# Two projections whose low weight halves are made by two engines: GpSimd beside the vector engine

## The chip, the cores and the metric

The kernel runs on one core of one Trainium2 chip. A core has five engines with a queue of instructions each: TensorE (PE in the profile) for matrix products, VectorE (DVE) and ScalarE (ACT) for element-wise work, GpSimd (POOL), and SyncE (SP), which here only issues DMAs. They meet at semaphores. The metric is the device time of one execution in microseconds (us): the median before is 1877.37 us over 3 runs (1877.23 to 1877.73).

## The reference

Two layers run one after the other on a sequence of 256 tokens with 2048 channels, all in float32. Cut to what matters:

```python
def hybrid_layer(x, ...):
    h = rmsnorm(x, norm_g)
    proj = h @ w_in                       # one wide input projection, then split
    y_conv = conv_branch(...) @ w_proj_conv
    y_mla = mla_branch(...) @ w_proj_mla
    y = sigmoid(g_conv) * y_conv + sigmoid(g_mla) * y_mla
    return x + y @ w_out
```

The change touches the two last products of a layer: `w_proj_conv` (2048 by 2048) and `w_out` (2048 by 2048).

## The kernel before

**Split products.** Every float32 product is made of three passes on TensorE in a faster 4-byte format (F32R). An operand is cut into a high part, its rounding to F32R, and a low part, the difference between the value and its high part. With the activations as the stationary operand in parts `sh` and `sl`, and the weights as the moving operand in parts `hi` and `lo`, a block is the sum of `sh*hi`, `sl*hi` and `sh*lo`, accumulated in PSUM (line 314 chooses among them).

**Pieces.** Weights are streamed from memory in pieces, in the order in which they are used (`plan`, lines 161 to 173). A piece holds `KS = 2` K tiles of 128 rows, so it is 128 partitions by 1024 columns for a block 512 columns wide. A piece goes through three engines. `load` (line 182) issues its DMA on SP into a `raw` buffer, of which there are five. `split_hi` (line 191) lets ScalarE write the high part into one of four `hi` buffers. `split_lo` (line 211) lets VectorE write the low part into one of three `lo` buffers, as raw minus high, in one instruction over both K tiles.

**Blocks and slots.** `product` (line 294) makes one block of 256 tokens by 512 columns. In the two products of the change a block has K of 2048, so 16 K tiles and 8 pieces, and a piece feeds 12 matmuls of 512 columns: for two K tiles and two token tiles, the three parts. At piece i the code first issues the high parts up to piece i+3 and the low parts up to piece i+2, then the 12 matmuls of piece i, then `background(n)`, which moves a clock on by one slot and runs the steps that are due in it. `order_of_products` (line 280) puts the four low matmuls of a piece behind its eight high ones; the last piece of a block finishes token tile 0 first, and one piece of a block (`tardy`) takes its late activations in last. Since three `lo` buffers serve, the low part of piece i+2 goes into the buffer that TensorE has finished with at the end of piece i-1.

**Order.** Each engine is wrapped in `InOrder` (line 118), so that it executes in the order in which the code issues. A step that is put off by `at_slot` is issued behind the matmuls of a later piece, and what is issued in a queue before it goes first.

**What GpSimd does.** It issues most of the DMAs that turn a block's result by way of memory: `park` (line 327) writes a tile of 128 by 512 with four DMAs, `fetch` (line 336) reads it back with one, and VectorE finishes with a 32 by 32 transposition. After a block of the convolution's projection (`pconv_evac`) VectorE multiplies and adds two tiles, and each is parked with four DMAs on GpSimd and fetched. After a block of the output projection in the first layer (`wout_evac`) it is the same, with one more DMA for each tile that writes x for the second layer. In the second layer `wout_evac` writes the output with four DMAs on GpSimd instead. In the last block of each product (c = 3) the second tile's park is issued on SP, and the evacuation comes one slot sooner, since the next product waits for it: its last two pieces (pieces 6 and 7 of block 0, where `tardy=6`) read those activations. GpSimd also computes the small inverse square roots of attention, earlier in the layer.

**Names.** In the profile `acc` is a PSUM block; `raw`, `hi`, `lo` are the pieces' buffers; `ycT` are the activations of the convolution's projection, `yT` those of the output projection, `hT` those of the second layer; `gate` and `xres` are tiles on their way out, `turn_d` is the memory they are parked in, `turned` the tile fetched. All instructions have line 126, that of the `InOrder` wrapper.

Of the kernel before, what the change touches and what calls it, by code (L numbers as in the profile page):

```python
# [11 lines left out]
F32 = mybir.dt.float32  # L12
# [93 lines left out]
def blocks_of_layer():  # L106

    s = {"win": [], "wuq": [], "wukv": [], "wpc": [], "wpm": [], "wo": []}
    for kind, i, stream in order_of_layer():
        s[stream].append(DOWN_BLOCKS[i][1] if kind == "down" else 2 * QK if kind == "uq" else 512)  # L110
    return s
# [3 lines left out]
def trunk(ctx: ExitStack, tc: tile.TileContext, xT, x, g_in, pos, win, wuq, wukv, wpc, wpm, wo, cst, rows, invf, out):  # L115
# [19 lines left out]
    pe, vec, act, gps, sp = (InOrder(e) for e in (nc.tensor, nc.vector, nc.scalar, nc.gpsimd, nc.sync))  # L135
# [20 lines left out]

    streams = {"win": (win, 16), "wuq": (wuq, 4), "wukv": (wukv, 4), "wpc": (wpc, 16), "wpm": (wpm, 16), "wo": (wo, 16)}
    taken = {}
    pieces = []

    def plan(layer, stream):
        ap, nk = streams[stream]
        i, at = taken.get((layer, stream), (0, 0))
        n = blocks_of_layer()[stream][i]
        mine = []
        for g in range(nk // KS):
            size = P * KS * n
            pieces.append((ap[layer, at : at + size].rearrange("(p k c) -> p k c", p=P, k=KS), n))
            at += size
            mine.append(len(pieces) - 1)  # L170
        taken[layer, stream] = (i + 1, at)
        return nk, n, mine

# [2 lines left out]
    for l in range(DEPTH):  # L176
        plans.append([(k, i, plan(l, s)) for k, i, s in order_of_layer()])

    loaded, highs, done, blocks_begun = {}, {}, {}, [0]
# [11 lines left out]
    def split_hi(i):  # L191
        if i >= len(pieces) or i in highs:
            return
        load(i)
        highs[i] = split_p.tile([P, KS, pieces[i][1]], F32R, tag="hi", name=f"hi{i}", bufs=4)
        singly = i < 2
        for a in range(0, KS, 1 if singly else KS):
            k = slice(a, a + 1 if singly else KS)

            for step in ("h", "w"):  # L200
                if step == "w":
                    act.copy(highs[i][:, k], loaded[i][:, k])
                    if singly:
                        split_lo(i, k)
                elif i * KS < NCT:
                    for c in range(i * KS + k.start, i * KS + k.stop):
                        first_h(c)
        for a in range(1, LOAD_AHEAD + 1):
            load(i + a)

    def split_lo(i, k=slice(0, KS)):
        if i >= len(pieces) or done.get(i, (0, 0, 0))[2] >= k.stop:
            return
        lo = done[i][1] if i in done else split_p.tile([P, KS, pieces[i][1]], F32R, tag="lo", name=f"lo{i}")
        vec.tensor_sub(lo[:, k], loaded[i][:, k], highs[i][:, k].bitcast(F32))
        done[i] = highs[i], lo, k.stop


# [75 lines left out]
    def product(planned, stat, evacuate, evac_at=EVAC_AT, costs=(0.0, 0.0), before=None, tardy=None):  # L294
        nk, n, mine = planned
        blocks_begun[0] += 1
        pts = [acc_p.tile([P, 512], F32, tag=f"acc{blocks_begun[0] % 2}{t}", name=f"acc{mine[0]}_{t}") for t in range(T)]

        def evac():
            for t in range(T):  # L300
                evacuate(t, pts[t][:, :n])

        for j, i in enumerate(mine):
            for a in range(HI_AHEAD + 1):
                split_hi(i + a)
                if a <= LO_AHEAD:
                    split_lo(i + a)
            hi, lo, _ = done[i]
            if before:
                before(j)  # L310
            for t, kk, part in order_of_products(i, j == len(mine) - 1, j == tardy):
                k = j * KS + kk
                sh, sl = stat(k, t)
                stationary, w = ((sh, hi), (sl, hi), (sh, lo))[part]
                pe.matmul(
                    pts[t][:, :n], stationary, w[:, kk, :],
                    start=k == 0 and part == 0, stop=k == nk - 1 and part == 2,
                )
            if j == len(mine) - 1:
                steps.insert(0, (clock[0] + 1 + evac_at, costs, evac))  # L320
            background(n)
# [1023 lines left out]
```

## Time and profile before

| | |
|---|---|
| median of the runs | 1877.37 us (3 runs, 1877.23 to 1877.73) |
| span of the profiled execution, first to last instruction | 1876.2 us |
| VectorE busy | 1577.1 us (84%) |
| ScalarE busy | 1366.1 us (73%) |
| GpSimd busy | 484.9 us (26%), 942 instructions |
| low parts on VectorE | 690 instructions, 815.2 us |

The profiled execution was not timed apart from its profile; its span of 1876.2 us lies 1.2 us below the median, which also holds what lies around the first and the last instruction. Times in the profile's timelines count from the span's start. A row of a timeline gives start, duration, engine, operation, the tile written and the tiles read, and in square brackets how long the engine sat idle before and what ended the wait. Rows of neighbouring instructions of one kind are merged, with their count behind an x. A matmul of 512 columns is issued 0.227 us after the one before it and shows some 0.39 us, since they overlap in the engine.

### The profile page before, as it was taken

To read this page: it belongs to the slowest core of one execution; us is meant where nothing else is said; L and a number is where in the kernel's file an instruction comes from. 1 tells how busy PE (TensorE), PEld (TensorE's weight loads), DVE (VectorE), ACT (ScalarE), POOL (GpSimd) and SP (SyncE) were. 2 spreads that over 40 slices of the span, in tenths; PEclk is the share of its full clock that TensorE was granted. 3 is DMA by queue.
4 is the path that set the end of the run, shared out by engine and by line. 5 is a ranking of instruction groups with operands and counts; after the bars stand their busy time and mean duration, and the time that the engine had idled before them with its cause. 6 is when DMAs were issued, how large, how long until landed. Compare 5 with 4: busy or idle time off the path is not lost.

```text
span 1876.2 us, 27388 instructions
## 1 busy us (share of the span) xinstructions
PE 1871.3 (100%) x8665; PEld 1584.0 (84%) x8665; DVE 1577.1 (84%) x2426; ACT 1366.1 (73%) x2468; POOL 484.9 (26%) x942
## 2 busy tenths in 40 slices
PE   9999999999999999999999999999999999999999
PEld 8988888888888888888899888888888888888887
DVE  6898988989999988766679899888899999885664
ACT  7678988888888766544557688888888878474442
POOL 1055555432200000122221555555322000001210
PEclk9999999999999999999999999999999999999999
DMA  9677878777755566678876787787777555566774
GB/s 329 217 258 263 273 240 275 262 242 235 244 201 193 196 206 214 210 241 281 288 234 218 249 272 258 261 278 243 245 239 249 190 194 203 209 205 221 239 250 164
DMA packets 140113, 445.06 MB, mean 237 GB/s; under 512 B 23808, under 2 KB 29440, under 8 KB 139968
## 3 DMA queue, kind: packets, MB, share of 16 engines
q1 hardware_dynamic: 106272, 359.89, 57.1%
q0 software_dynamic: 32832, 82.62, 13.5%
q8 instruction: 68, 1.11, 0.2%
q10 hardware_dynamic: 864, 0.80, 0.1%
q14 instruction: 77, 0.63, 0.1%
HBM read 399.18 MB, written 44.04 MB: 236 GB/s over the span
## 4 chain that ended last, share of the span: by engine, by line
PE 100%; DVE 0%; DVEq 0%; issue 0%
PE acc L126 97%; PE s L126 2%; PE o_ps L126 1%; PE warm L126 0%; PE var L126 0%; PE mu L126 0%; DVE xres L126 0%; DVEq L1341 0%; DVE zeros L126 0%
## 5 line engine op out<-in xcount | busy, mean ns | idle before, releaser
L126 ACT CAST hi<-raw 128x1024 fp32r<-128x1024 f32 (+3 forms) x690 | 700.7, 1021 | 408.4 <-PE acc L126 348.1
L126 DVE TENSOR_TENSOR lo<-raw,hi 128x1024 fp32r<-128x1024 f32 (+3 forms) x690 | 815.2, 1183 | 197.7 <-PE acc L126 151.1
L126 PE MATMUL acc<-hi,hT 128*128 128x512 f32 (+2 forms) x1728 | 419.5, 382 | 0.0
L126 PEld LDWEIGHTS acc<-hi,hT 128*128 128x128 f32 x1728 | 319.8, 188 | 59.2
L126 PE MATMUL acc<-hi,h_hi 128*128 128x512 f32 (+2 forms) x864 | 260.7, 383 | 0.0
L126 PE MATMUL acc<-hi,h_lo 128*128 128x512 f32 (+2 forms) x864 | 260.5, 383 | 0.0
L126 ACT ACTIVATE tap<-u_t,cst 128x256 f32<-128x256 f32 x588 | 254.7, 499 | 3.2 <-DVE v_t L126 3.2
L126 PE MATMUL acc<-lo,h_hi 128*128 128x512 f32 (+2 forms) x864 | 229.8, 382 | 0.0
L126 PE MATMUL acc<-lo,hT 128*128 128x512 f32 (+2 forms) x864 | 229.3, 382 | 0.0
L126 DVE TENSOR_TENSOR v_t<-v_t,tap 128x512 f32<-128x512 f32 x294 | 202.2, 688 | 10.4 <-ACT hi L126 0.5
L126 POOL DMA_DIRECT2D turned<-turn_d x88 | 49.1, 558 | 536.6 <-DVE v_t L126 305.4
L126 PEld LDWEIGHTS acc<-hi,h_lo 128*128 128x128 f32 x864 | 161.4, 188 | 30.2
L126 PEld LDWEIGHTS acc<-lo,h_hi 128*128 128x128 f32 x864 | 160.9, 188 | 30.0
L126 PEld LDWEIGHTS acc<-lo,hT 128*128 128x128 f32 x864 | 160.6, 188 | 29.9
L126 PEld LDWEIGHTS acc<-hi,h_hi 128*128 128x128 f32 x864 | 160.4, 188 | 29.0
L126 POOL DMA_DIRECT2D turn_d<-gate x184 | 100.0, 551 | 327.8 <-DVE gate L126 182.9
L126 DVE SCALAR_TENSOR_TENSOR v_t<-u_t,cst,v_t 128x256 f32<-128x256 f32 x372 | 159.7, 480 | 2.3
L126 PE MATMUL acc<-hi,oT 128*128 128x512 f32 x512 | 127.8, 389 | 0.0
L126 PE MATMUL acc<-hi,ycT 128*128 128x512 f32 x512 | 127.7, 389 | 0.0
L126 PE MATMUL acc<-hi,yT 128*128 128x512 f32 x512 | 127.7, 389 | 0.0
L126 PE MATMUL acc<-hi,qkc 128*128 128x512 f32 (+1 forms) x512 | 118.7, 363 | 0.0
L126 PEld LDWEIGHTS acc<-hi,ycT 128*128 128x128 f32 x512 | 96.1, 188 | 19.9
(169 smaller groups left out, 2209.8 us busy)
## 6 DMA issues: line engine op xcount, KB each, us to landing
raw<-in_win SPq DMA_DIRECT2D x382, 512.0 KB, 4.3
raw<-in_wpm SPq DMA_DIRECT2D x64, 512.0 KB, 3.2
raw<-in_wpc SPq DMA_DIRECT2D x64, 512.0 KB, 4.3
raw<-in_wo SPq DMA_DIRECT2D x64, 512.0 KB, 4.8
raw<-in_wukv SPq DMA_DIRECT2D x32, 512.0 KB, 3.6
turned<-turn_d POOLq DMA_DIRECT2D x56, 256.0 KB, 4.8
raw<-in_win SPq DMA_DIRECT2D x32, 384.0 KB, 4.4
raw<-in_wuq SPq DMA_DIRECT2D x32, 384.0 KB, 3.4
```

Source lines behind the costliest of these rows:

```text
L126: ins = getattr(self.engine, name)(*a, **k)
```

## The change

The pieces of `wpc` (the weights of the convolution's projection) and `wo` (those of the output projection) are noted in a set `shared`. For those pieces the low part is made by two instructions of 128 by 512: GpSimd subtracts in the first K tile, VectorE in the second. That is 32 pieces for each of the two products in each of two layers, 128 in all. The other streams' low parts stay one VectorE instruction over both K tiles.

```diff
-    pieces = []
+    pieces, shared = [], set()
...
             mine.append(len(pieces) - 1)
+            if stream in ("wpc", "wo"):
+                shared.add(len(pieces) - 1)
...
         lo = done[i][1] if i in done else split_p.tile([P, KS, pieces[i][1]], F32R, tag="lo", name=f"lo{i}")
-        vec.tensor_sub(lo[:, k], loaded[i][:, k], highs[i][:, k].bitcast(F32))
+        if i in shared:
+            for engine, a in ((gps, 0), (vec, 1)):
+                engine.tensor_sub(lo[:, a], loaded[i][:, a], highs[i][:, a].bitcast(F32))
+        else:
+            vec.tensor_sub(lo[:, k], loaded[i][:, k], highs[i][:, k].bitcast(F32))
         done[i] = highs[i], lo, k.stop
```

The order of instructions on TensorE and ScalarE stays as it was. On VectorE each of the 128 instructions stands where it stood, at half its width. On GpSimd 128 subtractions are new in the queue, among the DMAs: the queue of one block of the output projection in the first layer reads 8 parks, 2 writes of x, 4 subtractions, 2 fetches, 4 subtractions; behind the last block of the convolution's projection it reads 4 parks, 2 subtractions, 2 fetches.

## The prediction

> **What bounds the kernel now.** I read the page first, then what TensorE waits for, then the busy time of the engines in the two stages of the change, then the timeline at their edges.
>
> ```profile
> span 1876.2 us, 27388 instructions
> ...
> PE 1871.3 (100%) x8665; PEld 1584.0 (84%) x8665; DVE 1577.1 (84%) x2426; ACT 1366.1 (73%) x2468; POOL 484.9 (26%) x942
> ...
> PEclk9999999999999999999999999999999999999999
> ...
> PE warm L126 <- DVE zeros L126: 1.2, 1, 1.2
> ...
> 764.90:851.90 87.00, 87.00 (x385) 72.07 (x384) 56.47 (x64) 40.39 (x44) 16.45 (x30) 1.00 0.72 230
> 851.90:939.00 87.10, 87.10 (x386) 72.14 (x385) 56.48 (x71) 44.16 (x64) 23.05 (x42) 1.00 0.85 284
> ```
>
> TensorE is busy 1871.3 of 1876.2 us at the full granted clock (1.00 in both stage rows, whose columns are the stretch, its length, then PE, PEld, DVE, ACT and POOL busy). It waits once in the whole run, 1.2 us at the start; the rest of the 4.9 us without matmuls is the end, behind the last one. The two stages of the first layer, the convolution's projection and the output projection, last 87.0 and 87.1 us with TensorE never idle. So relief of the vector engine buys nothing: whatever changes here shows only if it makes TensorE wait.
>
> **What is removed and what is added.**
>
> ```profile
> L126 DVE TENSOR_TENSOR lo<-raw,hi 128x1024 fp32r<-128x1024 f32 x32 | 38.8, 1221 | 28.2 <-PE acc L126 25.3 <-issue 2.8
> ...
> L126 DVE TENSOR_TENSOR lo<-raw,hi 128x512 fp32r<-128x512 f32 x4 | 2.8, 689 | 0.0
> ```
>
> The groups of VectorE in the first stage, and the same operation at half width elsewhere (name, count, busy us, mean ns, idle time before and its causes): 128 vector instructions shrink from 1.221 to 0.689 us, 68 us of busy time in all. Before, VectorE sat 25.3 of 87 us waiting for TensorE to free a `lo` buffer: it was ahead already. Worth to the path: 0.
>
> GpSimd takes 128 subtractions of 128x512. No such instruction is in the trace; the nearest rows:
>
> ```profile
> L126 POOL TENSOR_TENSOR rsq_t<-r_p x48: 193/313/1173, 133.2 to 1307.4; 128x8 f32<-128x8 f32 x48
> ...
> L126 POOL MEMSET u_t<- 128x60 f32 x16 | 2.7, 167 | 0.3 <-POOLq L1334 0.3
> L126 POOL MEMSET qk_t<- 128x512 f32 x2 | 1.1, 548 | 0.0
> ```
>
> Two memsets give (548-167)/452 = 0.843 ns a column; a two-input operation of 8 columns takes 193 ns when nothing holds it up. From these, estimates for 512 columns: 193 ns and 504 columns at one pass, 0.62 us, the lower bound; two reads in turn, 1.04 us; two reads and a write in turn, 1.47 us, the upper bound. I take 1.25 us, midway between the last two, since no row shows two reads at once, nor that the write can't overlap.
>
> The Trainium skill, GPSIMD Engine Reference, section Elementwise — side-by-side cycle accounting, gives 4497 ns for 2048 columns of a two-input add; a quarter is an estimate of 1.12 us, and by it the sum below would come to about 1878.5. Its section Engine selection speaks against the change: two-input element-wise work belongs on VectorE, GpSimd being about twice as slow; no run here shows it yet.
>
> The first row's 193/313/1173 (least, median, most) says that the price isn't fixed. The timeline shows why:
>
> ```profile
> 133.19 0.19 POOL L126 TENSOR_TENSOR rsq_t<-r_p 128x8 f32<-128x8 f32 x1 [2.10 <-DVE r_p L126]
> ...
> 134.11 1.23 DVE L126 TENSOR_TENSOR lo<-raw,hi 128x1024 fp32r<-128x1024 f32 x1 [0.34 <-issue]
> ...
> 134.32 1.07 POOL L126 TENSOR_TENSOR rsq_t<-r_p 128x8 f32<-128x8 f32 x1
> ```
>
> The same small operation takes 0.19 us alone and 1.07 us when it comes just behind VectorE's subtraction, ending with that one (134.11+1.23 = 135.34, 134.32+1.07 = 135.39). So GpSimd's subtraction will wait for a vector subtraction that is under way. Here both halves are freed by the same matmul, so they meet at every piece: 0.69+1.25 = 1.94 us for the two one after the other. Whether VectorE waits in the same way behind GpSimd the trace doesn't show; I count with both orders.
>
> The Trainium skill, SBUF — State Buffer, section Who interferes with whom, says that whichever starts first holds the shared read port for its whole instruction, so VectorE would wait too; were it never to wait, the late-first order below would fall away and the sum would be 1878.2.
>
> **Inside a block it is hidden.** A piece is 12 matmuls, 2.72 us, and the low part's matmuls come two pieces and eight matmuls behind the release of their buffer:
>
> ```profile
> 873.90 1.98 PE L126 MATMUL acc<-hi,yT 128*128 128x512 f32 x8
> ...
> 876.27 4.37 POOL L126 DMA_DIRECT2D turn_d<-xres  x8 [16.68 <-DVE xres L126]
> 876.62 1.98 PE L126 MATMUL acc<-hi,yT 128*128 128x512 f32 x8
> ...
> 881.02 1.11 POOL L126 DMA_DIRECT2D x_dram<-xres  x2 [0.38 <-DMA turn_d<-xres]
> ...
> 883.87 1.07 PE L126 MATMUL acc<-lo,yT 128*128 128x512 f32 x4
> ...
> 874.16 1.23 DVE L126 TENSOR_TENSOR lo<-raw,hi 128x1024 fp32r<-128x1024 f32 x1 [1.55 <-issue]
> 875.30 1.28 DVE L126 TENSOR_TENSOR xres<-acc,xres 128x512 f32<-128x512 f32 x2
> ```
>
> A buffer freed at 876.62 is read as low part at 883.87: 7.25 us. Its subtraction starts 0.26 us behind the release (873.90 to 874.16) and both halves end 1.94 us later, so 5.05 us are spare. That cover is gone only where GpSimd's queue holds the subtraction back.
>
> **Behind an evacuation** it does. In the output projection of layer 0 the subtraction freed at 876.62 stands behind 8 parks and 2 writes of x, which end at 881.02+1.11 = 882.13; two more such blocks follow (the fourth's subtractions are over by then). With VectorE's half first, the adds into `xres` come 0.53 us sooner, GpSimd's earlier subtraction ends at 874.85+1.25 = 876.10, the parks start there instead of at 876.27, and our subtraction ends at 882.13-0.17+1.25 = 883.21: 0.66 us spare. With GpSimd first, VectorE's half ends at 874.16+1.25+0.69 = 876.10, the first add at 876.74, the parks start 0.33 us later as now (875.94 to 876.27), all 0.80 us later than before: the subtraction ends at 884.18, 0.3 us late, and 1.0 us late if VectorE's next half holds it for 0.69 us. Bounds 0 and 1.0 us for each of three; I take 0.25: no row tells which goes first, and one of the two orders costs nothing. The convolution's projection has only the 8 parks, which end 1.1 us sooner against the deadline, and layer 1's output has 4 DMAs: 0 there. A gap like this one would add up to 1.4 us to a window (2.07-0.66):
>
> ```profile
> 838.28 1.63 POOL L126 DMA_DIRECT2D turn_d<-gate  x3 [2.07 <-issue]
> ```
>
> Throughput fits too, by GpSimd's groups in the two stages.
>
> ```profile
> L126 POOL DMA_DIRECT2D turn_d<-gate x24 | 13.1, 552 | 72.6 <-DVE gate L126 70.5 <-issue 2.1
> L126 POOL DMA_DIRECT2D turned<-turn_d x6 | 3.4, 566 | 11.2 <-DMA turn_d<-gate 11.0
> ...
> L126 POOL DMA_DIRECT2D turn_d<-xres x24 | 13.1, 553 | 42.0 <-DVE xres L126 42.0
> L126 POOL DMA_DIRECT2D turned<-turn_d x8 | 4.4, 556 | 10.9 <-DMA turn_d<-xres 7.2 <-DVE yT L126 3.1 <-DVE lo L126 0.6
> L126 POOL DMA_DIRECT2D x_dram<-xres x6 | 3.4, 564 | 0.7 <-DMA turn_d<-xres 0.7
> ```
>
> A block lasts 8 x 2.72 = 21.77 us. Its DMAs cost 8 x 0.552 + 2 x 0.566 = 5.55 us in the convolution's projection, leaving 2.03 us a subtraction; 6.66 and some 0.38 of waiting in layer 0's output, leaving 1.84. At 1.25 and half of VectorE's 0.69 as the mean wait, 1.60, both hold.
>
> **At the change of product.** Two subtractions now stand between the last park and the fetches that output block 0 needs for pieces 6 and 7.
>
> ```profile
> 853.14 2.20 POOL L126 DMA_DIRECT2D turn_d<-gate  x4 [8.67 <-DVE gate L126]
> ...
> 858.47 1.13 POOL L126 DMA_DIRECT2D turned<-turn_d  x2 [3.13 <-DVE yT L126]
> ...
> 866.92 0.62 ACT L126 CAST yT<-turned 128x512 fp32r<-128x512 f32 x1 [0.93 <-DVE turned L126]
> ...
> 867.91 1.28 DVE L126 TENSOR_TENSOR yT<-turned,yT 128x512 fp32r<-128x512 f32 x2
> 868.46 1.07 PE L126 MATMUL acc<-hi,yT 128*128 128x512 f32 x4
> ...
> 870.27 2.43 PE L126 MATMUL acc<-hi,yT 128*128 128x512 f32 x10
> ```
>
> The parks end at 855.34, the subtractions at 857.84, and the fetches, which waited until 858.47 for a buffer in any case, lose nothing; if VectorE's half and its two `yT` subtractions go first (3 x 0.69), they start at 859.91, 1.44 us late. The second cast ends at 867.54 and is read at 868.46+2x0.227 = 868.91, 1.37 us spare; the second `yT` low part ends at 869.19 and is read at 870.27+0.45, 1.53 us spare, from which a GpSimd subtraction freed at 868.46 can take 1.25. Bounds 0 and 1.44+1.25-1.53 = 1.2 us; I take 0.4, once in each layer. The second layer's start has no subtraction on GpSimd ahead of its fetches.
>
> **Sum.** 3 x 0.25 + 2 x 0.4 = 1.55 us on the path. The profiled execution spans 1876.2 us, 1.2 below the median; on its terms 1877.8, on the median's 1877.37+1.55 = 1878.9 us. Upper bounds give 3 x 1.0 + 2 x 1.2 = 5.4, and at 1.47 us a subtraction some 1.5 more: 1884.
>
> **The rivals.** *GpSimd can't keep up.* Decided from 1.84 us a subtraction, its waits included, in layer 0's output and 2.03 in the convolution's projection: the queue then never catches up, and the blocks run at its pace. At 2.1: 8 x 2.1 + 5.55 - 21.77 = 0.58 us a block, 2.3 in four blocks, and 2.03 a block, 8.1, in layer 0's output; the first 5.05 of a layer are spare, so 5.4 remains, with the windows' 5.4 it is 1888. At 2.5: 3.78 us for each of eight blocks and 5.27 for each of four, 51, less the two spares of 5, 1918. For it: the 1.07 us of a tiny operation, and an unmeasured F32R result; against it: even the upper bound of 1.47 with the mean wait makes 1.82. Chance 0.25.
>
> *All is hidden.* VectorE goes first everywhere, spares of 0.66 and 1.4 us suffice: 1877.4. The same time comes if GpSimd always holds VectorE up, so that the relief is not one. Chance 0.12.
>
> *Faster.* Only the 4.9 us at the ends are left, and neither holds a shared piece. 1873.6 at the least gain that counts; chance 0.03.
>
> **How the numbers follow.** The forecast, small exposed waits, has 0.60, with its own range 1877.4 to 1884; 0.16 of it lies above 1881.1. A difference under 0.2% (3.75 us) counts as none, about what a measurement of this kernel can tell. Within: 0.12 + 0.44 = 0.56; slower: 0.25 + 0.16 = 0.41; faster 0.03. The range 1877.0 to 1890 leaves out the faster case and the 0.15 of the first rival above 1890.
>
> **What would show it.** Right: the GpSimd subtraction's least time is near 1.25 us and its median under 1.9; TensorE's waits name GpSimd's `lo` a few times, each under 1 us, behind evacuations of layer 0's output and in block 0. Wrong: a shared stage much over 87.1 us, GpSimd busy nearly all of it; or waits at every piece, which would mean the subtraction's price; or no wait at all.

## The result, and the profile after

The changed kernel takes 1882.44 us (median of 10 runs, 1881.77 to 1883.29); the kernel before, run beside it, 1877.8 us (10 runs, 1877.23 to 1878.66). The ratio is 1.0025, with a 95% interval of 1.0016 to 1.0034: 4.6 us slower, just over the 0.2% that counts (the interval reaches below it), and inside the predicted range.

The page of the changed kernel, the waits of TensorE (us in total, times, longest), the groups of GpSimd and VectorE, and the busy time in the four shared stages (stretch, length, PE, PEld, DVE, ACT, POOL):

```profile
span 1880.4 us, 27901 instructions
...
PE 1872.3 (100%) x8665; PEld 1582.1 (84%) x8665; DVE 1567.8 (83%) x2426; ACT 1366.4 (73%) x2468; POOL 682.8 (36%) x1070
```

```profile
PE acc L126 <- POOL lo L126: 1.7, 3, 0.7
PE warm L126 <- DVE zeros L126: 1.2, 1, 1.2
PE acc L126 <- DVE lo L126: 0.9, 2, 0.5
PE acc L126 <- ACT hi L126: 0.5, 1, 0.5
```

```profile
L126 POOL TENSOR_TENSOR lo<-raw,hi 128x512 fp32r<-128x512 f32 x128 | 198.6, 1562 | 124.0 <-PE acc L126 75.2 <-ACT hi L126 33.6 <-POOL lo L126 9.8
...
L126 DVE TENSOR_TENSOR lo<-raw,hi 128x512 fp32r<-128x512 f32 x132 | 135.2, 1036 | 136.6 <-PE acc L126 122.9 <-issue 6.8 <-POOL lo L126 6.1
```

```profile
764.90:852.00 87.10, 85.94 (x378) 70.48 (x378) 54.99 (x64) 40.37 (x43) 64.27 (x62) 1.00 0.66 222
852.00:941.00 89.00, 88.01 (x387) 72.24 (x386) 58.00 (x71) 43.51 (x63) 66.67 (x73) 1.00 0.82 276
1701.30:1789.30 88.00, 87.53 (x387) 72.13 (x386) 51.33 (x53) 37.14 (x39) 68.50 (x62) 1.00 0.69 226
1789.30:1876.40 87.10, 87.10 (x386) 72.02 (x384) 39.66 (x56) 32.77 (x33) 58.24 (x48) 1.00 0.67 213
```

TensorE now waits in three of the four shared stages, five times in all, three times for GpSimd's half and twice for VectorE's. The wait for ScalarE's `hi` lies at 11 us, before any shared piece. The halved vector instruction should last 0.69 us and lasts 1.04 on average, so VectorE is held up, and its 68 us of relief have shrunk to 9.3 (1577.1 to 1567.8).

From the starts of successive matmuls, less the usual 0.227 us and with the slow one behind each wait, the five gaps are 0.73 us at 822, 0.97 at 842, 0.83 at 886, 0.70 at 909 and 0.74 at 1780: 2.44 us in the convolution's projection, 1.53 in layer 0's output, 3.97 together. The wait at 11 us adds 0.8. Each of the five lies behind an evacuation. Two of them, read in the timeline (start, duration, engine, what; in brackets the idle time before and its cause), the first:

```profile
811.75 4.38 POOL L126 DMA_DIRECT2D turn_d<-gate  x8 [0.84 <-DVE gate L126]
...
814.49 6.00 DVE L126 TENSOR_TENSOR yT<-turned,yT 128x512 fp32r<-128x512 f32 x2
...
816.14 5.50 POOL L126 TENSOR_TENSOR lo<-raw,hi 128x512 fp32r<-128x512 f32 x4
...
820.41 2.98 DVE L126 TENSOR_TENSOR lo<-raw,hi 128x512 fp32r<-128x512 f32 x3
821.39 0.39 PE L126 MATMUL acc<-lo,ycT 128*128 128x512 f32 x1
...
822.24 0.96 PE L126 MATMUL acc<-lo,ycT 128*128 128x512 f32 x3 [0.46 <-DVE lo L126]
```

Here GpSimd is not the late one. Behind the eight parks four subtractions have piled up, and GpSimd runs them one behind the other. VectorE's two subtractions for `yT` take 1.28 us in the kernel before:

```profile
815.00 1.28 DVE L126 TENSOR_TENSOR yT<-turned,yT 128x512 fp32r<-128x512 f32 x2
```

Now they take 6.00 us, since the second lasts 5.40. Narrower windows of the changed kernel's timeline part the two runs of rows, and show when VectorE comes in:

```profile
816.14 3.79 POOL L126 TENSOR_TENSOR lo<-raw,hi 128x512 fp32r<-128x512 f32 x3
818.92 1.05 ACT L126 CAST hi<-raw 128x1024 fp32r<-128x1024 f32 x1 [1.66 <-PE acc L126]
819.97 1.67 POOL L126 TENSOR_TENSOR lo<-raw,hi 128x512 fp32r<-128x512 f32 x1
820.41 1.77 DVE L126 TENSOR_TENSOR lo<-raw,hi 128x512 fp32r<-128x512 f32 x1
```

GpSimd's first three subtractions follow one another without a stop, until 819.93. The fourth starts at 819.97, just as ScalarE's cast for it ends (818.92 + 1.05), so GpSimd had to wait for it. There VectorE's `yT` subtraction gets in and ends at 820.49; GpSimd's fourth then lasts 1.67 us in place of some 1.29. VectorE's first half of a piece, queued behind, waits in turn for that fourth one, lasts 1.77 us and ends at 822.19, and the second low matmul, due at 821.39 + 0.23, waits for it. The second window:

```profile
877.90 4.40 POOL L126 DMA_DIRECT2D turn_d<-xres  x8
...
883.95 1.12 POOL L126 DMA_DIRECT2D x_dram<-xres  x2 [1.66 <-DMA turn_d<-xres]
884.26 0.69 DVE L126 TENSOR_TENSOR lo<-raw,hi 128x512 fp32r<-128x512 f32 x1 [2.03 <-PE acc L126]
885.09 3.78 POOL L126 TENSOR_TENSOR lo<-raw,hi 128x512 fp32r<-128x512 f32 x3
...
886.44 1.19 PE L126 MATMUL acc<-lo,yT 128*128 128x512 f32 x4 [0.56 <-POOL lo L126]
```

Here GpSimd is late itself, as predicted for this window. The writes of x waited 1.66 us for the landing of a park (0.38 in the profile of the kernel before), and the subtraction behind them starts at 885.09.

### The profile page after: what moved, and what is told of

Read it like the earlier page. It is cut to its first block, busy times and chain, and to the rows that moved or that the text cites. A ratio compares the mean times of both kernels' runs of the same rounds, so it can differ in the third digit from the quotient of the medians.

```text
span 1880.4 us, 27901 instructions
## 1 busy us (share of the span) xinstructions
PE 1872.3 (100%) x8665; PEld 1582.1 (84%) x8665; DVE 1567.8 (83%) x2426; ACT 1366.4 (73%) x2468; POOL 682.8 (36%) x1070
## 3 DMA queue, kind: packets, MB, share of 16 engines
q8 instruction: 68, 1.11, 0.2%
## 4 chain that ended last, share of the span: by engine, by line
PE 51%; DVE 0%; issue 0%; DVEq 0%
PE acc L126 50%; PE s L126 1%; PE o_ps L126 0%; DVE lo L126 0%; DVE xres L126 0%; DVEq L1347 0%; PE var L126 0%; PE mu L126 0%; DVEq L126 0%
## 5 line engine op out<-in xcount | busy, mean ns | idle before, releaser
L126 DVE TENSOR_TENSOR lo<-raw,hi 128x1024 fp32r<-128x1024 f32 (+3 forms) x690 | 791.6, 1150 | 214.3 <-PE acc L126 162.6
L126 POOL TENSOR_TENSOR lo<-raw,hi 128x512 fp32r<-128x512 f32 x128 | 198.6, 1562 | 124.0 <-PE acc L126 75.2
```

Source lines behind the costliest of these rows:

```text
L126: ins = getattr(self.engine, name)(*a, **k)
```

## The experiments

All were run against the kernel before on the same chip. "Over" is the difference of the medians; the gaps are those behind evacuations, from the matmuls' starts.

| run | us | over | ratio, 95% interval | gaps, us |
|---|---|---|---|---|
| the change | 1882.44 | 4.6 | 1.0025 (1.0016 to 1.0034) | 0.73, 0.97, 0.83, 0.70, 0.74 |
| conv_only | 1881.13 | 3.3 | 1.0018 (1.0009 to 1.0027) | 0.74, 0.97, 0.73, 0.74 |
| out_only | 1879.88 | 1.9 | 1.0009 (1.0000 to 1.0018) | 0.98, 0.50 |
| spare_fourth | 1878.03 | 0.2 | 1.0001 (0.9992 to 1.0010) | 0.28 (and 0.45 at a change of product) |
| parks_on_sync | 1878.04 | 0.2 | 1.0001 (0.9993 to 1.0010) | none (0.8 at the second layer's start) |
| x_on_sync | 1880.74 | 2.7 | 1.0014 (1.0005 to 1.0023) | 0.73, 0.96, 0.73 |
| no_reads | 1878.47 | 0.7 | 1.0004 (0.9995 to 1.0013) | 0.40 |
| no_reads_long | 1879.02 | 0.9 | 1.0006 (0.9997 to 1.0015) | 0.99 |
| pause | 1886.97 | 8.9 | 1.0050 (1.0036 to 1.0064) | seven, 0.4 to 1.7 |
| quarter | 1879.36 | 1.3 | 1.0007 (0.9998 to 1.0016) | 0.32, 0.48 |
| all_gps | 1932.62 | 54.6 | 1.0293 (1.0279 to 1.0307) | many, up to 6.8 |

### Where it is lost: one product at a time

```diff
-            if stream in ("wpc", "wo"):
+            if stream == "wpc":
```

> Only the convolution's projection (wpc) is shared; the output projection's low parts are VectorE's alone. Theory of places: the changed kernel loses time at five places, three of them in the convolution's projection (0.73, 0.97 and 0.74 us by the matmuls' start times), so 2.4 us over the kernel before, with TensorE waits only behind evacuations of that product. Rival, a cost spread over all 128 pieces (a semaphore or port price at each): 64 pieces, half of 4.64, 2.3 us, but then without gaps of 0.7 us at three places.

```diff
-            if stream in ("wpc", "wo"):
+            if stream == "wo":
```

> Only the output projection (wo) is shared. Theory of places: the two gaps that the changed kernel had in layer 0's output projection (0.83 and 0.70 us), 1.5 us over the kernel before, none in layer 1, whose evacuations issue 4 DMAs and no parks. Rival, a cost spread over the 64 pieces: 2.3 us, as much in layer 1 as in layer 0.

The gaps stand in the places named, and in the second run there is none in layer 1, as a cost spread over the pieces would need. The sizes fit less well: conv_only has a fourth gap, at 1757, which the changed kernel does not have, and the two together (5.2 us) come to more than the change. In that window of the changed kernel both `yT` subtractions get through before GpSimd's run; the instruction caught is the half behind them, and it is in time. In conv_only the second `yT` subtraction is caught:

```profile
1752.16 4.87 DVE L126 TENSOR_TENSOR lo<-raw,hi 128x512 fp32r<-128x512 f32 x1
```

```profile
1749.80 5.40 DVE L126 TENSOR_TENSOR yT<-turned,yT 128x512 fp32r<-128x512 f32 x1
```

The first line is from the changed kernel, the second from conv_only. What decides is small: the second `yT` subtraction starts 1.11 us ahead of GpSimd's first row in the changed kernel and 1.05 us ahead in conv_only.

The gaps account for 3.18 of 3.33 us and 1.48 of 1.85.

### Is it the place in GpSimd's queue?

The piece whose subtraction stands directly behind the parks, the fourth of each block, goes back to VectorE:

```diff
-            if stream in ("wpc", "wo"):
+            if stream in ("wpc", "wo") and g != 3:
```

> The fourth piece of each block (the one whose GpSimd subtraction stands directly behind the 8 parks of the block before) goes back to VectorE whole; the other seven are shared. Theory of the queue: the next piece has 2.72 us more, so all five gaps vanish, 0 to 0.5 us over the kernel before. Rival, a cost at every piece: 112 of 128 remain, 4.1 us. Rival, VectorE held up by GpSimd's run of subtractions: the run shrinks from four to three (5.5 to 4.1 us), so the two gaps on VectorE's half shrink by about 1.3 us each and vanish too, but VectorE's yT subtraction still takes over 2 us.

The parks of the first three blocks of each product leave GpSimd's queue, all subtractions stay:

```diff
             if c < 3:
-                return turn(src, 512, None, then=use, then_costs=costs)
+                return turn(src, 512, None, then=use, then_costs=costs, queue=sp)
```

> As the changed kernel, but the parks of the first three blocks of both products are issued on SyncE instead of GpSimd. Theory of the queue: no subtraction stands behind 8 parks, GpSimd never runs four of them back to back, the five gaps vanish, 0 to 0.5 us over the kernel before. If the two engines' meeting at every piece is the cause, nothing changes: 4.6 us. If loads behind the parks on SyncE come late, TensorE or ScalarE wait for raw instead.

The writes of x leave it, parks and subtractions stay:

```diff
-            late.append(lambda: gps.dma_start(x1_dram[t, :, c * 512 : (c + 1) * 512], xt))
+            late.append(lambda: sp.dma_start(x1_dram[t, :, c * 512 : (c + 1) * 512], xt))
```

> As the changed kernel, but the two writes of x behind each evacuation of layer 0's output projection are issued on SyncE. In the changed kernel they took 1.12 us of GpSimd's queue and 1.66 and 1.55 us of waiting there for the landing of the first park. Theory: without these 2.8 us the subtraction behind them is in time, the two gaps of the output projection vanish, those of the convolution's projection stay (0.73, 0.97, 0.74): 2.4 to 3.3 us over the kernel before. Rival, the 8 parks alone make it late, as in the convolution's projection: all five gaps stay, 4.6 us.

The first two cost 0.2 us, which the measurement can't tell from nothing, though 112 and 128 subtractions are still on GpSimd, at the same price and meeting VectorE at most pieces. So neither GpSimd's work nor the meeting costs time: what stands ahead of it in the queue does. VectorE is still held up in spare_fourth, but not long enough to be late:

```profile
L126 DVE TENSOR_TENSOR yT<-turned,yT x16: 676/681/3622, 814.9 to 1803.1; 128x512 fp32r<-128x512 f32 x16
```

One `yT` subtraction there lasts 3.62 us (least, median and most in ns: 676/681/3622), through a run of two in place of three. The third run takes away just the gaps of the output projection. There the two writes and their wait decide, as the prediction had it; in the convolution's projection eight parks alone are enough (for the gap at 842 with the stop of 2 us inside them), which it had not.

### Is VectorE held up by what GpSimd reads?

GpSimd writes its half with two memsets in place of the subtraction, in the same place of its queue; the low part of each first K tile is left out:

```diff
-            for engine, a in ((gps, 0), (vec, 1)):
-                engine.tensor_sub(lo[:, a], loaded[i][:, a], highs[i][:, a].bitcast(F32))
+            for _ in range(2):
+                gps.memset(lo[:, 0].bitcast(F32), 0.0)
+            vec.tensor_sub(lo[:, 1], loaded[i][:, 1], highs[i][:, 1].bitcast(F32))
```

> GpSimd's subtraction becomes two memsets of its half (2 x 0.55 us and a gap, some 1.2 us, which write but read nothing); the low part of each first K tile in wpc and wo is left out (zeros). Its place in the queue stays. If VectorE is held up by what GpSimd reads, the waits that TensorE had on VectorE's half (0.73 and 0.74 us in the convolution's projection) vanish, VectorE's subtractions stay at 0.69 us even beside GpSimd, and GpSimd, no longer held by VectorE either, ends earlier: 0 to 1.5 us over the kernel before, what is left being in the output projection. If lateness in GpSimd's queue alone is the cause, the gaps stay at five places, 3.5 to 4.6 us.

Two memsets take 1.11 us, less than the subtraction's 1.27, so the run leaves two readings: nothing is read, or the work is shorter. The next has three memsets (`range(3)`); in a row of four pieces they take 6.60 us, 1.65 each, where the subtraction takes 5.50, 1.37 each:

> As the run with memsets, but three of them instead of two: GpSimd's price is 1.6 us and more, above the subtraction's 1.27 alone and its 1.37 in a run of four; the low part of each first K tile in wpc and wo is left out. If VectorE's late halves come from what GpSimd reads, VectorE's subtractions stay at 0.69 us, its yT subtraction too, and the two gaps on VectorE's half (0.73 and 0.74) do not come back although GpSimd's run of four lasts longer (6.6 us); gaps on GpSimd's own half may come back, behind the writes of x (up to 0.5 us each) and behind the park that an issue gap of 2 us splits (1.2 us): 0 to 2.5 us over the kernel before. If the shorter price was what helped with two memsets, all five gaps are back and larger: 4.6 us or more.

The least, median and most of VectorE's `yT` subtractions, in ns, in the changed kernel and, below, with three memsets; then TensorE's waits with three memsets:

```profile
L126 DVE TENSOR_TENSOR yT<-turned,yT x16: 677/680/5408, 814.5 to 1805.8; 128x512 fp32r<-128x512 f32 x16
```

```profile
L126 DVE TENSOR_TENSOR yT<-turned,yT x16: 680/682/685, 813.8 to 1802.5; 128x512 fp32r<-128x512 f32 x16
```

```profile
PE warm L126 <- DVE zeros L126: 1.2, 1, 1.2
PE acc L126 <- POOL lo L126: 0.7, 1, 0.7
```

With GpSimd writing alone, VectorE is not held at all, and the gaps on VectorE's half stay away although GpSimd is busy longer than in the change. The parks don't hold it either: here too the second `yT` subtraction runs beside the last of them (814.43 to 815.12, GpSimd's first memset starts at 815.43). Left is the one window in which the parks themselves stop for 2 us without a visible cause. So those two gaps come from the subtraction itself, and not from its place or its length. A memset differs from it by reading nothing; an operation with one input, which would part one read from two, was not run.

If a VectorE instruction waits until GpSimd pauses, a pause behind each subtraction should let it in:

```diff
                 engine.tensor_sub(lo[:, a], loaded[i][:, a], highs[i][:, a].bitcast(F32))
+            gps.memset(tick, 0.0)
```

> As the changed kernel, with a memset of 8 columns (0.1 us) on GpSimd behind each of its subtractions. In the changed kernel a VectorE subtraction waited 5.4 us, through three GpSimd subtractions that followed one another without a pause, and went on in the first pause. If a pause lets it in, no yT subtraction lasts over 2.1 us (0.69 and one of GpSimd's), and the two gaps on VectorE's half vanish; the three on GpSimd's half stay or grow by 0.1 to 0.7 us, since VectorE now goes first: 2 to 4 us over the kernel before. If a pause of that size is no opening, or the wait has another cause, yT still takes 5 us and the time is 4.6 to 5.5 us over.

Neither expectation came true: the cost is 8.9 us. The timeline behind the same evacuation:

```profile
815.50 7.37 DVE L126 TENSOR_TENSOR yT<-turned,yT 128x512 fp32r<-128x512 f32 x2
...
817.14 1.30 POOL L126 TENSOR_TENSOR lo<-raw,hi 128x512 fp32r<-128x512 f32 x1
...
818.37 0.12 POOL L126 MEMSET tick<- 128x8 f32 x1
818.43 1.30 POOL L126 TENSOR_TENSOR lo<-raw,hi 128x512 fp32r<-128x512 f32 x1
```

A memset of 0.12 us is no opening. VectorE now waits through four subtractions, not three, and takes 7.37 us for its two. What let it in at 819.93 in the changed kernel was, by the rows, that GpSimd's fourth subtraction had to wait for ScalarE's cast; here GpSimd's four subtractions and their memsets follow one another without a wait. Where the two start together, GpSimd also comes first at most pieces, so that VectorE's half lasts 1.78 us there (the one at 806.63, 0.05 us behind GpSimd's, for example). In the change VectorE goes first at most of them, by 0.03 to 0.04 us; this order is that close.

### The price

GpSimd makes 256 columns and VectorE 768:

```diff
-            for engine, a in ((gps, 0), (vec, 1)):
-                engine.tensor_sub(lo[:, a], loaded[i][:, a], highs[i][:, a].bitcast(F32))
+            flat = lambda t: t.rearrange("p k c -> p (k c)")
+            for engine, s in ((gps, slice(0, 256)), (vec, slice(256, None))):
+                engine.tensor_sub(flat(lo)[:, s], flat(loaded[i])[:, s], flat(highs[i])[:, s].bitcast(F32))
```

> GpSimd makes 256 of a piece's 1024 columns, VectorE 768 in one instruction. Price on GpSimd, from 0.19 us at 8 columns and 1.27 at 512: 0.73 us. A run of four behind the parks shrinks from 5.0 to 2.9 us and its first ends 0.54 us sooner, so gaps of 0.73, 0.97, 0.74, 0.83 and 0.70 us shrink to 0.1 to 0.4 or vanish: 0 to 1.2 us over the kernel before. Rival, a fixed price for each meeting of the engines: 4.6 us.

GpSimd makes all 1024:

```diff
-            for engine, a in ((gps, 0), (vec, 1)):
-                engine.tensor_sub(lo[:, a], loaded[i][:, a], highs[i][:, a].bitcast(F32))
+            gps.tensor_sub(lo, loaded[i], highs[i].bitcast(F32))
```

> GpSimd makes the whole low part of the shared pieces, VectorE nothing of them. Price: 2 x 1.27 less one start of 0.1, 2.45 us. Theory of throughput: a block of 21.77 us leaves 2.03 us a subtraction beside its DMAs in the convolution's projection and 1.84 in layer 0's output, so GpSimd can't keep up: (8 x 2.45 + 5.55 - 21.77) = 3.4 us for each of eight blocks, 4.9 for each of four, less 5 us spare in each layer: some 36 us over the kernel before, 1914. Rival, only the windows behind evacuations come 1.2 us later each: 9 to 12 windows, 18 us at most, 1896.

GpSimd's subtraction in the change, at a quarter, and whole (least, median and most in ns):

```profile
L126 POOL TENSOR_TENSOR lo<-raw,hi x128: 1273/1672/1820, 760.0 to 1868.7; 128x512 fp32r<-128x512 f32 x128
```

```profile
L126 POOL TENSOR_TENSOR lo<-raw,hi x128: 727/1516/1539, 760.4 to 1865.8; 128x256 fp32r<-128x256 f32 x128
```

```profile
L126 POOL TENSOR_TENSOR lo<-raw,hi x128: 2327/2402/2935, 760.1 to 1919.4; 128x1024 fp32r<-128x1024 f32 x128
```

Least times of 0.73, 1.27 and 2.33 us lie on a line of 2.1 ns a column. The medians show what the meeting does: at a quarter VectorE's longer half (0.955 us) goes first and GpSimd's median is twice its least. At a quarter the cost falls to 1.3 us, a little above what was expected; its interval holds zero, but two gaps remain. Whole, at 2.4 us, GpSimd can't keep up any more, and 54.6 us are lost, 19 us more than worked out from GpSimd's own time:

```profile
PE acc L126 <- POOL lo L126: 25.3, 11, 4.6
PE acc L126 <- DVE yT L126: 12.5, 2, 6.3
```

12.5 us of it are two waits of TensorE, up to 6.3 us each, for VectorE's `yT` at the change of product, which GpSimd shuts out. These waits and those for GpSimd's half are 37.8 us together. Most of the rest is TensorE itself running slower behind the long waits. Two stretches that begin at the end of a wait, or just after it (columns as above; the value behind POOL is TensorE's granted clock):

```profile
851.00:857.00 6.00, 6.00 (x22) 4.80 (x22) 0.00 (x0) 1.65 (x2) 6.00 (x3) 0.79 0.67 206
933.50:939.50 6.00, 6.00 (x15) 4.75 (x16) 0.00 (x0) 1.45 (x2) 6.00 (x3) 0.55 0.58 185
```

In the first of them matmuls start 0.427 us apart in place of 0.227. The trace has six such stretches, each beginning within 1.3 us of a gap of 2.8 us or more; the mean clock of the run is 0.992, against 1.000 in the profiles of all the other runs. By the matmuls' starts in the four shared stages and the start of the second layer, gaps over 0.7 us cost 39.6 us and slow matmuls 14.1 us. So the long waits cost more than their own length, which the expectation of 36 us didn't have.

### The wait at the start

> The kernel before, profiled once more. In the profiles of the changed kernel and of most others TensorE waits 0.3 to 0.7 us for ScalarE at 11 to 12 us, where the code is the same in all of them; the first profile of the kernel before shows no such wait. If that is how loads at the start vary from one execution to the next, a second profile may show it here too or not, and the gaps behind evacuations are absent again. If the wait is the change's, it stays absent here.

The kernel before, profiled once more, took 1878.2 us. The wait is there too (0.4 us for `hi`, a gap of 0.69 at 11.6 us), with no other gap. One profile of the kernel before has it and one has not, so it varies between executions. That leaves up to 0.7 us in the differences of the table that the gaps behind evacuations do not explain.

## Why the prediction was right, and where it was not

**What holds.** TensorE bounds the kernel and VectorE's relief buys nothing: with the subtractions out of the way of the parks, half of the low parts move to GpSimd at 0.2 us. The price of 1.25 us was right (1.27 at least). The estimate from the Trainium skill, GPSIMD Engine Reference, section Elementwise — side-by-side cycle accounting, a quarter of 4497 ns or 1.12 us, was a little low. VectorE goes first at most pieces, by 0.03 us, so the dear order didn't come. No piece inside a block is late. The own range of the forecast, 1877.4 to 1884, holds the time, near its upper end.

**What was luck.** The sum came to 1.55 us and the cost to 4.6, three times as much. The range holds it because the bounds left room in windows that cost less or nothing, at the change of product above all, while more than half of the gaps' 3.97 us came from windows that were put at 0. A difference of under 0.2% had the larger chance, 0.56; it came out at 0.25%, on the side that had 0.41.

**The windows of layer 0's output were too small a term.** 3 x 0.25 us were taken, two gaps of 0.83 and 0.70 came, within the bound of 1.0. The price and the order were right; the wait of the writes of x, taken over from the kernel before as 0.38 us, was 1.66 and 1.55 in the two windows with a gap, and 0.64 in the third, which has none. Without the writes both gaps are gone. The longer wait is not the change's: the second profile of the kernel before has it in the first of these windows, where the first profile had 0.38.

```profile
882.54 1.12 POOL L126 DMA_DIRECT2D x_dram<-xres  x2 [1.66 <-DMA turn_d<-xres]
```

So this wait differs between executions of one kernel, and a single profile gave its low value as if it were fixed. With 1.66 in place of 0.38, the prediction's spare of 0.66 us becomes 0.62 us too late, and the matmul waited 0.72 us (0.83 with the slow one behind). What makes the park land later in one execution than in another stays open.

**The convolution's windows were put at 0, and cost 2.44 us.** This step failed. It let VectorE wait for one GpSimd subtraction at most, and looked only at whether GpSimd's half would be in time. The runs show that a backlog of four subtractions shuts VectorE out until GpSimd first has to wait, here through three of them, and the next VectorE instruction through the fourth, so that VectorE's half comes late while GpSimd's does not. The Trainium skill, SBUF — State Buffer, section Who interferes with whom, has the second engine wait until the first one's instruction ends. That agrees with single meetings (1.82 us for GpSimd's subtraction beside VectorE's half, 1.28 alone) but not with a run: the 5.4 us last through three instructions. The third gap there came from the stop of some 2 us inside the parks. The prediction had quoted its row, which lies in this very projection, but added it to no window there; it is in both profiles of the kernel before (2.07 and 2.06 us), and again here:

```profile
839.06 1.63 POOL L126 DMA_DIRECT2D turn_d<-gate  x3 [2.04 <-issue]
...
842.04 1.20 PE L126 MATMUL acc<-lo,ycT 128*128 128x512 f32 x4 [0.70 <-POOL lo L126]
```

**The changes of product cost nothing,** where 2 x 0.4 us were taken (one wait of this kind, 0.45 us for ScalarE's `yT`, came in spare_fourth): the fetches start 0.3 us later against TensorE (858.47 before at a start of 852.14, 860.59 now at some 854.0), and the spare of 1.37 us covers it.

**The rivals.** GpSimd's mean of 1.56 us with waits stays under 1.84 and 2.03, so it keeps up. At 2.4 it doesn't, as that rival had it; the size worked out for it, 36 us, was too small. (In the rival's own sum at 2.1 us a subtraction, 2.03 us a block should read 2.07: 8 x 2.1 + 6.66 + 0.38 - 21.77.) That all is hidden holds only with the queue cleared. Nothing became faster, here or in any run.

## What to carry to other kernels

When work moves to an engine that also issues DMAs, look not at its busy time but at what stands ahead of the moved instruction in its queue, and compare the end of that with the moment the result is read. A backlog then does harm twice: GpSimd's two-input instructions ran back to back here and shut VectorE's two-input instructions out until GpSimd had to wait for something, so the engine that was relieved can be the one that comes late. Take a wait that a spare depends on from more than one profile: here it was 0.38 us in one and 1.66 in the other. Before moving work off an engine, see whether anything waits for it; here nothing did, and the best that any variant reached was the time before.

## What the runs showed of the hardware beyond expectation

A VectorE subtraction with both inputs in SBUF waited 5.4 us through three GpSimd subtractions and 6.8 us through four with a memset of 0.1 us between each; GpSimd's memsets of 0.53 us never held it (least to most 680 to 685 ns with three memsets). VectorE instructions with one input in PSUM are not held either, as the same stretch of the changed kernel shows beside GpSimd's subtraction of 809.09 to 810.91:

```profile
809.09 1.82 POOL L126 TENSOR_TENSOR lo<-raw,hi 128x512 fp32r<-128x512 f32 x1 [0.91 <-POOL lo L126]
809.66 0.68 DVE L126 TENSOR_TENSOR gate<-acc,sc 128x512 f32<-128x512 f32 x1
810.38 1.07 DVE L126 TENSOR_TENSOR gate<-gate,ym 128x512 f32<-128x512 f32 x1
```

The product with a PSUM input takes its usual 0.68 us, the sum of two SBUF tiles 1.07 in place of 0.69, until GpSimd ends. One thing stays open: the `yT` subtraction that was shut out starts at 815.1, and at its usual 0.68 us would have been over before GpSimd's first row at 816.14. The parks that GpSimd issues meanwhile are not the reason, as the run with three memsets shows. So GpSimd seems to shut VectorE out about 1 us before its row begins: a `yT` subtraction that starts 1.05 us ahead of that row is caught (815.09 against 816.14), and one that starts 1.11 us ahead goes through (1751.55 against 1752.66). This was not tried in a run of its own.
